# All four token tiles pass each stage of the layer together, and 66 blocks of the product with U run ahead of the first V block

## The chip, the cores and the metric

The kernel runs on one core of one Trainium2 chip. The metric is the device time of that core in microseconds. Of the kernel before three runs are shown: 1733.40, 1733.98 and 1734.52 us, median 1733.98.

## What is computed

One decoder layer of width 1024 on 512 tokens. Sub-layer 1 is a modulated norm, an input projection whose columns go to two groups of eight attention heads (a latent attention with rotary keys, and a forgetting attention), and an output projection. Sub-layer 2 is a product-key expert mixer, and nearly all of the time is spent there or on the way to it. Cut to what matters:

```python
h = modulate(x, norm1_g, shift1, scale1);  proj = h @ w_in            # 1024 wide
o = concat(latent_attention(proj), forgetting_attention(proj))        # 8 + 8 heads, causal
x = x + gate1 * (o @ w_o)
h2 = modulate(x, norm2_g, shift2, scale2)
qp = (h2 @ w_pq)                        # 8 heads x 2 halves x 128
sc = einsum("bshpd,hpnd->bshpn", qp, sub_keys)        # 128 keys for each half
s1, i1 = top_k(sc[..., 0, :], 16);  s2, i2 = top_k(sc[..., 1, :], 16)
top_s, top_c = top_k(s1[..., :, None] + s2[..., None, :], 16)
expert = i1[top_c // 16] * 128 + i2[top_c % 16];  gate = softmax(top_s)
a = einsum("bcd,bchkd->bchk", h2, peer_u[expert])     # 16384 experts x 1024
y = einsum("bchk,bchkd->bcd", gate * gelu(a), peer_v[expert])
x = x + gate2 * y
```

## The kernel before, in words

The 512 tokens are four tiles of 128. All products that need fp32 are made of three matmuls (`mm3`, L405): each operand is split into a rounded part `hi` and a rest `lo`. A weight is loaded in pieces of 128x1024; ScalarE casts `whi` (L397), and VectorE or GpSimd subtracts to `wlo` (L398). The `halves` of a weight are kept under the number of the pair of tiles (`i // 2`), so each weight is loaded and split once for tiles 0 and 1 and again for tiles 2 and 3.

The front has, for each tile: `hidden` (the norm, transposed), the base projections (`latent_q`, `latent_k`, `fox_qk` twice, `fox_v`; L409 to L411) and `mla_tile` (L193), sixteen `head`s (score L590, softmax, transposes L156, product with V L605), `out_proj`, `hidden2`. Then `queries` (with `w_pq`; L409 to L411 with `h2hi`) give the scores against the keys (L676 on), and `best` takes the sixteen best of 128 keys for each half (five VectorE instructions, L733 to L737). `choose` calls `select`, the pick: sums of candidates (L763), again a top-16, and a look-up of the expert's number (L779 on VectorE, L781 on GpSimd, L782 on VectorE).

Of the four tiles, three are dense and one is sparse. For the dense tiles `gate_matrix` turns the numbers and gates into a matrix G over all 16384 experts: one-hots on VectorE (L821 to L824), products on TensorE (L830), written to DRAM. Then all experts are computed, in 128 blocks of 128: `dense_u` (24 matmuls 128x384, L929 to L931, with `ut` split by `split`, L883 and L884) and `gelu` give `ge`, and `v_in` and `v_mm` multiply it by the gate (L962), split it (`whl`, L965, L966) and add 18 matmuls 128x512 (L975). A U block must come before its V block; `AHEAD = 20` blocks go first and the rest alternate with V. For the sparse tile, 3, `sparse_steps` gathers rows of U and V from DRAM (L841) and works on VectorE alone: 128 u-steps (L862) and 128 v-steps (L871), a few beside each V block.

Every engine takes its own instructions in order. That order comes from generators: `pipe` starts a task every few rounds, `weave` puts a number of steps of a second generator between steps of a first. The last part of `build` (L1070 to L1095) is the plan: tiles 0 and 1 up to their scores; then the picks and gates of tiles 0 and 1 as `fill` beside base projections and heads of tiles 2 and 3; then the output projections and queries of these; then picks and gates of tile 2 beside the first U blocks.

Of the kernel before, what the change touches and what calls it, by code (L numbers as in the profile page):

```python
# [21 lines left out]
P = 128  # L22
# [4 lines left out]
H = 8  # L27
# [19 lines left out]
AHEAD = 20  # L47
# [33 lines left out]
class Layer:  # L81
    def __init__(self, ctx, tc, I, out):
# [26 lines left out]

    def q4(self, shape, name, dt=F32):  # L110
        return self.q4p.tile(list(shape), dt, name=name, tag="q4")
# [84 lines left out]
    def setup(self):  # L196
# [25 lines left out]
        self.mask = cp.tile([P, S], F32, name="mask")  # L222
# [32 lines left out]
    def rope_tables(self):  # L255
# [34 lines left out]
        self.rope = {}  # L290
        for j, name in enumerate("qk"):
            g1 = rg[:, j * RD:j * RD + hf][:, None, :].to_broadcast([P, NT, hf])
            g2 = rg[:, j * RD + hf:(j + 1) * RD][:, None, :].to_broadcast([P, NT, hf])
            c = cp.tile([P, NT, RD], F32, name="rc_" + name)
            s = cp.tile([P, NT, RD], F32, name="rs_" + name)
# [42 lines left out]
    def mod_cols(self, j, name, bias, gain=None, first=False, halves=(0, 1)):  # L338
# [3 lines left out]
        for half in halves:  # L342
            alloc = self.g8 if not first else self.q4 if half == 0 else self.oh if gain is None else self.l4
# [38 lines left out]
    def weights(self, i, name, alloc):  # L382

        if (i // 2, name) not in self.wt:
            self.wt[i // 2, name] = self.wload(self.I[name], alloc)
        return self.wt[i // 2, name]

    def halves(self, i, name, src, engs, new=None):

        if (i // 2, name) not in self.wt:  # L390
# [10 lines left out]
            self.wt[i // 2, name] = his.__getitem__, los.__getitem__  # L401
        return self.wt[i // 2, name]
# [749 lines left out]
```

## Time and profile before

| | |
|---|---|
| median of three runs | 1733.98 us (1733.40 to 1734.52) |
| the profiled run, its own time | 1733.38 us |
| its span | 1731.6 us |
| TensorE matmul busy | 1607.5 us, 93% |
| VectorE busy | 1315.4 us, 76% |
| ScalarE busy | 706.9 us, 41% |
| GpSimd busy | 649.0 us, 37% |
| DMA | 414.93 MB, mean 240 GB/s |

A row of a window gives the stretch in us from the span's start, its length, and for TensorE (PE), its weight loads (PEld), VectorE (DVE), ScalarE (ACT) and GpSimd (POOL) the busy time with the number of instructions in brackets; then the granted TensorE clock as a share of the full one, the mean busy share of the DMA engines, and GB/s. A window of one line gives only the engines on which that line has instructions. A row of a group gives line, engine, operation, operands out<-in with their shapes and the count, then busy time and mean duration of one in ns, then the idle time just before them and what ended it. Busy time counts a moment once; means of overlapping instructions add up to more.

### The profile page before, as it was taken

The numbers are of one execution on the slowest core, as the hardware profiler recorded it, in microseconds if no ns is written. First come the engines' busy times: TensorE is split into PE (matmuls) and PEld (weight loads), VectorE is DVE, ScalarE is ACT, GpSimd is POOL, SyncE is SP. The second block draws the span as 40 slices with busy tenths as digits, with TensorE's granted clock in tenths as the row PEclk, the third lists the DMA queues.
The fourth block names the chain that finished last, engine by engine and source line by source line (L and its number), as shares of the span: only waits on it lengthen the run. The fifth ranks groups of instructions, "written<-read, shape, count | busy, mean of one in ns | idle before, by whom it ended". The sixth has DMA issues, their size and how long they took to land.

```text
span 1731.6 us, 25066 instructions
## 1 busy us (share of the span) xinstructions
PE 1607.5 (93%) x9105; PEld 1417.4 (82%) x9105; DVE 1315.4 (76%) x2762; ACT 706.9 (41%) x1100; POOL 649.0 (37%) x569
## 2 busy tenths in 40 slices
PE   7999878789879789779999999999999999999998
PEld 3758877569758689768889999999999999999987
DVE  4735669989898987877888888888888877445764
ACT  3435544259465246633333333333333333333331
POOL 1650735641432440373554444534534433001200
PEclk8999989889989899889999999999999999999999
DMA  8584454325276436868999999999999999445761
GB/s 298 182 307 147 144 172 152 100 74 169 76 250 202 145 97 202 261 242 281 341 341 348 354 323 342 339 331 348 325 337 356 314 336 353 132 159 178 260 200 67
DMA packets 160909, 414.93 MB, mean 240 GB/s; under 512 B 13201, under 2 KB 68497, under 8 KB 159250
## 3 DMA queue, kind: packets, MB, share of 16 engines
q1 hardware_dynamic: 64658, 242.85, 40.7%
q0 software_dynamic: 37440, 137.38, 22.0%
q10 hardware_dynamic: 58688, 33.11, 6.5%
q8 instruction: 71, 1.16, 0.3%
q14 instruction: 52, 0.43, 0.1%
HBM read 380.25 MB, written 33.03 MB: 239 GB/s over the span
## 4 chain that ended last, share of the span: by engine, by line
PE 69%; DVE 18%; DMA 3%; issue 3%; POOL 2%; ACT 2%; ACTq 0%; POOLq 0%; DVEq 0%
PE acc L975 30%; PE bank L931 9%; PE bank L929 9%; PE bank L930 9%; DVE wlo L398 2%; DVE idf L782 2%; PE bank L590 2%; PE bank L830 1%; PE bank L156 1%; PE bank L605 1%; PE bank L410 1%; PE bank L411 1%; PE bank L409 1%; DVE ti L737 1%; DVE sc L735 1%
## 5 line engine op out<-in xcount | busy, mean ns | idle before, releaser
L975 PE MATMUL acc<-vhi,whl 128*128 128x512 f32 x1524 | 435.9, 396 | 0.0
L929 PE MATMUL bank<-hhi,uhi 128*128 128x384 f32 x1024 | 346.9, 339 | 9.2 <-DMA hhi<-hd 6.5
L931 PE MATMUL bank<-hhi,ulo 128*128 128x384 f32 x1024 | 346.9, 339 | 6.3 <-DVE ulo L884 3.9
L930 PE MATMUL bank<-hlo,uhi 128*128 128x384 f32 x1024 | 346.4, 338 | 0.8 <-DMA hlo<-hd 0.8
L975 PEld LDWEIGHTS acc<-vhi,whl 128*128 128x128 f32 x1524 | 286.5, 189 | 57.5 <-issue 0.5
L841 POOL DMA_INDIRECT gat<-in_peer_v,ids x128 | 164.6, 1286 | 324.9 <-DVE y L871 150.5
L883 ACT CAST uhi<-ut 128x1024 fp32r<-128x1024 f32 x129 | 135.4, 1051 | 304.2 <-PE bank L930 301.6
L975 PE MATMUL acc<-vlo,whl 128*128 128x512 f32 x762 | 240.0, 396 | 10.4 <-POOL vlo L884 10.4
L841 POOL DMA_INDIRECT gat<-in_peer_u,ids x128 | 164.6, 1286 | 199.0 <-DVE sact L862 182.0
L884 DVE TENSOR_TENSOR ulo<-ut,uhi 128x1024 fp32r<-128x1024 f32 x124 | 153.3, 1237 | 110.6 <-ACT uhi L883 108.6
L883 ACT CAST vhi<-vt 128x1024 fp32r<-128x1024 f32 x127 | 133.3, 1050 | 234.3 <-PE acc L975 205.4
L884 DVE TENSOR_TENSOR vlo<-vt,vhi 128x1024 fp32r<-128x1024 f32 x122 | 149.7, 1227 | 81.1 <-ACT vhi L883 77.6
L929 PEld LDWEIGHTS bank<-hhi,uhi 128*128 128x128 f32 x1024 | 194.0, 190 | 14.9 <-issue 7.0
L931 PEld LDWEIGHTS bank<-hhi,ulo 128*128 128x128 f32 x1024 | 194.2, 190 | 9.4 <-DVE ulo L884 5.4
L930 PEld LDWEIGHTS bank<-hlo,uhi 128*128 128x128 f32 x1024 | 194.2, 190 | 5.6 <-DMA hlo<-hd 1.3
L975 PEld LDWEIGHTS acc<-vlo,whl 128*128 128x128 f32 x762 | 144.4, 190 | 44.9 <-POOL vlo L884 11.3
L871 DVE SCALAR_TENSOR_TENSOR y<-gat,swgt,y 128x1024 f32<-128x1024 f32 x127 | 162.4, 1279 | 19.0 <-DMA gat<-in_peer_v,ids 19.0
L398 POOL TENSOR_TENSOR wlo<-w,whi 128x1024 fp32r<-128x1024 f32 (+2 forms) x45 | 112.8, 2516 | 155.5 <-ACT whi L397 130.8
L862 DVE CUSTOM_DVE_ANT_0 scr<-gat,h 128x1024 bf16<-128x1024 f32 x128 | 155.9, 1218 | 14.2 <-DMA gat<-in_peer_u,ids 12.0
L965 ACT CAST whl<-ge 128x384 fp32r<-128x384 f32 x113 | 57.6, 512 | 138.8 <-DVE ge L962 120.8
L397 ACT CAST whi<-w 128x1024 fp32r<-128x1024 f32 (+2 forms) x88 | 84.8, 994 | 53.0 <-DMA w<-in_w_pq 10.4
L832 ACT ACTIVATE gst<-bank 128x512 f32<-128x512 f32 x96 | 95.0, 1083 | 24.2 <-PE bank L830 17.4
(278 smaller groups left out, 2620.4 us busy)
## 6 DMA issues: line engine op xcount, KB each, us to landing
ut<-in_peer_uT SPq DMA_DIRECT2D x128, 512.0 KB
vt<-in_peer_v SPq DMA_DIRECT2D x127, 512.0 KB
G<-gst ACTq DMA_DIRECT2D x24, 1024.0 KB
w<-in_w_pq SPq DMA_DIRECT2D x32, 512.0 KB
w<-in_w_ada SPq DMA_DIRECT2D x24, 512.0 KB
w<-in_w_ada SPq DMA_DIRECT2D x12, 1024.0 KB
w<-G SPq DMA_DIRECT2D x16, 768.0 KB
gt<-G SPq DMA_DIRECT2D x16, 768.0 KB
```

The source lines that it names most:

```text
L397: self.nc.scalar.copy(hi, w)
L398: engs[k // 2 % len(engs)].tensor_tensor(out=lo, in0=w, in1=hi, op=OP.subtract)
L832: nc.scalar.activation(st[:, :, q + t4:q + t4 + 4].rearrange("p i t -> p t i"), pb.rearrange("p (t i) -> p t i", t=4), AF.Copy, scale=1.0 ...
L841: self.nc.gpsimd.indirect_dma_start(out=t, out_offset=None, in_=self.I[table], in_offset=bass.IndirectOffsetOnAxis(ap=ids[:, k:k + 1], axi ...
L862: v.tensor_tensor_reduce(out=scr, in0=u, in1=h2, op0=OP.mult, op1=OP.add, scale=1.0, scalar=0.0, accum_out=a[:, k:k + 1])
L871: v.scalar_tensor_tensor(out=self.y, in0=t, scalar=w[:, k:k + 1], in1=self.y, op0=OP.mult, op1=OP.add)
L883: nc.scalar.copy(hi, src)
L884: eng.tensor_tensor(out=lo, in0=src, in1=hi, op=OP.subtract)
L929: pe.matmul(A, uh[:, k, :], hh, start=(k == 0), stop=False)
L930: pe.matmul(A, uh[:, k, :], hl, start=False, stop=False)
L931: pe.matmul(A, ul[:, k, :], hh, start=False, stop=(k == KD - 1))
L975: self.nc.tensor.matmul(self.acc[t][half], w[:, ts], v[:, half * 512:(half + 1) * 512], start=(b == n == 0), stop=(b == NK - 1 and n == 2))
```

## The change

Weights are kept under their name alone, so each is loaded and split once (44 pieces of 128x1024 in place of 88), those of `w_in` and `w_pq` all on VectorE. All four tiles go through each stage together, and one pool of 28 buffers replaces four pools. The queries take four tiles at once: 384 matmuls of 512 columns in place of 768 of 256. The sixteen calls of `top` stand, one for each step of the queries, after the first five steps. Then the U blocks begin (`ahead`), one for every two steps of the six picks of tiles 0 to 2 and one for every step of their gates; 66 of them in place of 20 are made before the loop over V. The `ge` of blocks 15 to 65 is stored to DRAM (`ged`) and loaded again three V blocks ahead (`ge_in`). The loop over V takes 1 or 2 sparse steps per block up to block 60, and 3 from there (before: 1 up to block 15, then 2 or 3). All `ulo` and `vlo` splits are on VectorE (before, five of each on GpSimd).

```diff
 EARLY = 15
-AHEAD = 20
+AHEAD = 66
...
-        self.k4p = self.top.enter_context(tc.tile_pool(name="k4", bufs=12))
-        self.q4p = self.top.enter_context(tc.tile_pool(name="q4", bufs=8))
-        self.w4p = self.top.enter_context(tc.tile_pool(name="w4", bufs=4))
-        self.l4p = self.top.enter_context(tc.tile_pool(name="l4", bufs=4))
+        self.k4p = self.top.enter_context(tc.tile_pool(name="k4", bufs=28))
...
-    def halves(self, i, name, src, engs, new=None):
-
-        if (i // 2, name) not in self.wt:
...
+    def halves(self, name, src, engs, new=None):
+
+        if name not in self.wt:
             kd, n = src.shape[1:]
             his, los = [], []
             for k in range(0, kd, 2):
-                w = self.w4([P, 2, n], "w")
+                w = self.k4([P, 2, n], "w")
                 self.last_load = self.nc.sync.dma_start(w, src[:, k:k + 2, :])
-                hi, lo = (new or self.q4)([P, 2, n], "whi", F32R), self.l4([P, 2, n], "wlo", F32R)
+                hi, lo = (new or self.k4)([P, 2, n], "whi", F32R), self.k4([P, 2, n], "wlo", F32R)
                 self.nc.scalar.copy(hi, w)
                 engs[k // 2 % len(engs)].tensor_tensor(out=lo, in0=w, in1=hi, op=OP.subtract)
                 his += [hi[:, x, :] for x in range(2)]
                 los += [lo[:, x, :] for x in range(2)]
-            self.wt[i // 2, name] = his.__getitem__, los.__getitem__
-        return self.wt[i // 2, name]
+            self.wt[name] = his.__getitem__, los.__getitem__
...
-    def w_in(self, i, name):
-
-        v, g = self.nc.vector, self.nc.gpsimd
-        new = {"w_c0": self.oh, "w_c1": self.oh, "w_fq": self.k4, "w_fv": self.oh}.get(name) if i > 1 else None
-        return self.halves(i, name, self.I[name], (g, g, v) if i > 1 else (v, g), new)
+    def w_in(self, name):
+
+        return self.halves(name, self.I[name], (self.nc.vector,), self.oh if name in ("w_c1", "w_fq") else None)
...
-    def w_pq(self, i, c):
-        v, g = self.nc.vector, self.nc.gpsimd
-        return self.halves(i, f"w_pq{c}", self.I["w_pq"][c], (v,) if c == 0 else (v, g))
+    def w_pq(self, c):
+        return self.halves(f"w_pq{c}", self.I["w_pq"][c], (self.nc.vector,), self.oh if c % 2 else None)
...
-        qT = (self.oh([P, 4, n], "qpT", F32) if group[0] == 0 else self.k4([P, 4, n], "qpT"))
+        qT = [self.k4([P, 2, n], "qpT") for _ in range(2)]
         for j in range(4):
             pb = self.bank()
             self.mm3(pb[:, :n], [lambda k, z=z: w[z](k)[:, j * P:(j + 1) * P] for z in range(2)], h, KD)
-            self.ecopy(qT[:, j, :], pb[:, :n], j)
+            self.nc.scalar.copy(qT[j // 2][:, j % 2, :], pb[:, :n])
...
-            nc.gpsimd.tensor_tensor(out=lo, in0=src, in1=hi, op=OP.subtract)
+            nc.vector.tensor_tensor(out=lo, in0=src, in1=hi, op=OP.subtract)
...
-                late = i == DENSE[-1] and q
+                late = q
...
+    def ahead(self):
         self.ge = {}
         self.acc, self.vs = None, {}
         self.dense_h2()
-        u = AHEAD
         for b in range(AHEAD):
             self.dense_u(b)
             yield
+
+    def dense(self):
+
+        u = AHEAD
         for b in range(NK):
+            self.ge_in(b + 3)
             self.v_in(b)
...
-        return self.split(ut, "u", self.nc.gpsimd if b % 2 and b < 11 else self.nc.vector)
+        return self.split(ut, "u", self.nc.vector)
...
+        if EARLY <= b < AHEAD:
+            nc.sync.dma_start(self.ged[b - EARLY], self.ge.pop(b))
+
+    def ge_in(self, b):
+
+        if EARLY <= b < AHEAD:
+            self.ge[b] = self.k2([P, ND_T], "ge")
+            self.load(self.ge[b], self.ged[b - EARLY])
...
-        vh, vl = self.split(vt, x, nc.gpsimd if b < 5 else nc.vector)
+        vh, vl = self.split(vt, x, nc.vector)
...
-        h0, h1 = hiddens([0, 1])
+        every = list(range(NT))
+        hs = hiddens(every)
         for x in ("a1", "b1", "a2", "b2"):
             self.mods[x] = self.cp.tile([P, KD], F32, name=x)
         m = [f for half in range(2) for f in (self.mod_cols(0, "b1", 0, None, True, (half,)),
                                               self.mod_cols(1, "a1", 1, 4, True, (half,)))]
+        h0, h1 = hs[:2]
         for g in (m[0], h0, h1, m[1], m[0], m[2], m[1], m[3], m[2], m[3], h0, h1):
             next(g, None)
         self.tables()
-        weave(pipe(base([0, 1]) + self.heads(0, T) + self.heads(1, T), 3),
-              spread(seq(self.mod_row(2, "g1", 0, self.k4, self.g8), spill(), self.mod_cols(3, "b2", 2), self.mod_cols(4, "a2", 3, 5)), 2), 1, 8)
-        b23, o01 = base([2, 3]), outs([0, 1])
-        run(pipe(o01[:3] + hiddens([2, 3]) + o01[3:] + seconds([0, 1]) + b23[:4] + [prep(self.w_pq, 0, 0)], 3))
-        weave(seq(*scores([0, 1])), seq(top(0, 0), top(1, 0), idle(2), top(0, 1), top(1, 1), pick(0, 0), top(0, 2)), 1, 5)
-        fill = seq(top(1, 2), top(0, 3), pick(0, 1), top(1, 3), gates(0), pick(1, 0), pick(1, 1), gates(1))
-        weave(pipe(b23[4:] + self.heads(2, T) + self.heads(3, T), 2), fill, 1)
-        run(pipe(outs([2, 3]) + [prep(self.w_pq, 2, 0)] + seconds([2, 3]), 2))
-        weave(seq(*scores([2, 3])), seq(top(2, 0), top(3, 0), idle(2), top(2, 1), top(3, 1), pick(2, 0), top(2, 2)), 1, 5)
-        dense = self.dense()
-        next(dense)
-        weave(seq(top(2, 3), pick(2, 1)), dense, 1, 0, 1, False)
-        for _ in range(4):
-            next(dense)
-        weave(gates(2), dense, 1, 1, 2, False)
-        sparse = seq(top(3, 2), top(3, 3), behind(pick(3, 0)), behind(pick(3, 1)), self.sparse_steps(SPARSE))
+        weave(pipe(hs[2:] + base(every) + self.heads(0, T) + self.heads(1, T), 3),
+              spread(seq(self.mod_row(2, "g1", 0, self.k4, self.g8), spill(), self.mod_cols(3, "b2", 2), self.mod_cols(4, "a2", 3, 5)), 2), 1, 10)
+        o = outs((0, 0), (1, 0), (2, 0), (0, 1), (1, 1), (2, 1), (3, 0), (3, 1))
+        run(pipe(self.heads(2, T) + self.heads(3, T) + o + [prep(self.w_pq, 0)] + seconds(every), 2))
+        tops = [top(i, c) for c in range(4) for i in every]
+        weave(seq(*scores(every)), seq(*tops), 1, 5)
+        ahead = self.ahead()
+        next(ahead)
+        weave(seq(*(pick(i, hh) for i in DENSE for hh in range(2))), ahead, 1, 0, 2, False)
+        weave(seq(*(gates(i) for i in DENSE)), ahead, 1, 0, 1, False)
+        run(ahead)
+        sparse = seq(behind(pick(3, 0)), behind(pick(3, 1)), self.sparse_steps(SPARSE))
         g2 = spread(self.mod_row(5, "g2", 1, self.o4, self.o4, True), 5)
-        for n, _ in enumerate(dense):
-            for _ in range(1 if n < 16 else 3 if n % 2 else 2):
+        for n, _ in enumerate(self.dense()):
+            for _ in range(3 if n >= AHEAD - 5 else 1 + n % 2):
                 next(sparse, None)
```

What this does to the order of VectorE's instructions shows at two places. The first is where the first U block's rest, `ulo` (L884 before, L870 after), stands among candidates (L733 to L737 before, L719 to L723 after, `sc` scores), look-ups (`lk`, `idf`) and one-hots (L807 to L810 after). Before:

```order
L763 TENSOR_TENSOR cand<-tv 128x4x2 x3
L734 MAX_INDEX ti<-tv,sc 128x8
L737 MAX_INDEX ti<-tv,sc_6360 128x8
L884 TENSOR_TENSOR ulo<-ut,uhi 128x1024
L779 TENSOR_TENSOR lk<-io_299,tpf 128x800
L734 MAX_INDEX ti<-tv,sc 128x8 x3
L735 MATCH_REPLACE sc_6366<-tv,sc 128x128
L782 TENSOR_REDUCE idf<-lk 128x16
L736 MAX tv<-sc_6366 128x8
```

And after, at the first `ulo`:

```order
L768 TENSOR_REDUCE idf<-lk 128x16
L723 MAX_INDEX ti<-tv,sc_4484 128x8
L809 TENSOR_TENSOR vhi<-vt,e_5577 128x1024
L810 TENSOR_TENSOR vhi<-vt,e_5577 128x1024
L722 MAX ts<-c_5451 128x8
L809 TENSOR_TENSOR vhi<-vt,e_5577 128x1024
L810 TENSOR_TENSOR vhi<-vt,e_5577 128x1024
L870 TENSOR_TENSOR ulo<-ut,uhi 128x1024
L770 CAST ids_4876<-idf 128x64
L765 TENSOR_TENSOR lk<-io_291,tpf 128x800
L870 TENSOR_TENSOR ulo<-ut,uhi 128x1024
```

Before, the first top-16s of tiles 2 and 3 stand on both sides of the first `ulo`, and those of tiles 0 and 1 far ahead of it. After, all 64 first top-16s (the last ends with the `MAX_INDEX` of `sc_4484`), 24 second ones (`c`), 16 look-ups and five steps of one-hots stand ahead of it. By TensorE's order 68 U blocks stand ahead of the first V matmul, behind one group of 16 one-hot matmuls (before, 24 by the trace).

The second place is VectorE in the loop over V: before, one V block with its U block and three sparse steps (L862 is a u-step, an `ISA` of two instructions, L871 a v-step):

```order
L871 SCALAR_TENSOR_TENSOR y<-gat,swgt,y 128x1024
L884 TENSOR_TENSOR vlo<-vt,vhi 128x1024
L862 ISA scr,sact<-gat,h_8273 128x1024
L862 ISA sact 128x1
L966 TENSOR_TENSOR whl<-ge,whl 128x384
L871 SCALAR_TENSOR_TENSOR y<-gat,swgt,y 128x1024
L884 TENSOR_TENSOR ulo<-ut,uhi 128x1024
L962 TENSOR_TENSOR ge<-ge,w_10735 128x192
L962 TENSOR_TENSOR ge<-ge,w_10736 128x192
L862 ISA scr,sact<-gat,h_8273 128x1024
L862 ISA sact 128x1
```

And after, between V block 6 and 60 (L870 is the split, L848 and L857 the sparse steps, L960 and L964 the gate and `whl`):

```order
L960 TENSOR_TENSOR ge<-ge,w_9914 128x192
L960 TENSOR_TENSOR ge<-ge,w_9915 128x192
L870 TENSOR_TENSOR vlo<-vt,vhi 128x1024
L848 ISA scr,sact<-gat,h_8939 128x1024
L848 ISA sact 128x1
L964 TENSOR_TENSOR whl<-ge,whl 128x384
L857 SCALAR_TENSOR_TENSOR y<-gat,swgt,y 128x1024
```

The `ulo` is gone from there, since U blocks 0 to 69 stand ahead of V block 6 and the next comes at V block 60, and each V block comes with one u-step and one v-step. From V block 78 on the order is that of before.

## Rows read from the trace of the kernel before

**Rows 1.** The whole span, cut into stages, all engines (windows).

```profile
0.00:227.00 227.00, 193.93 (x1103) 146.19 (x1103) 123.30 (x328) 108.35 (x245) 95.64 (x111) 0.94 0.63 220
20.00:200.00 180.00, 164.61 (x948) 124.23 (x941) 106.87 (x279) 90.27 (x204) 77.12 (x79) 0.96 0.60 211
227.00:592.70 365.70, 308.95 (x2366) 276.60 (x2365) 334.04 (x1070) 183.46 (x296) 154.29 (x143) 0.93 0.45 141
592.70:738.20 145.50, 128.70 (x836) 122.53 (x837) 119.89 (x347) 73.85 (x93) 40.11 (x48) 0.92 0.62 194
738.20:1731.60 993.40, 975.94 (x4805) 872.11 (x4804) 738.17 (x1020) 341.19 (x466) 359.01 (x269) 0.99 0.81 287
```

**Rows 2.** Queries and first top-16s: count, ns min/median/max, first and last start.

```profile
L409 PE MATMUL bank<-h2hi,whi x256: 278/283/561, 227.0 to 579.9; 128*128 128x256 f32 x128
...
L733 DVE MAX8 tv<-sc x64: 266/274/296, 244.6 to 589.1; 128x8 f32<-128x128 f32 x64
```

**Rows 3.** The chain in the steady stretch: start, us, what.

```profile
1463.60 4.18 PE acc L975 x18
...
1471.97 4.18 PE acc L975 x18
```

**Rows 4.** TensorE's timeline, runs of small matmuls: start, us, what.

```profile
164.78 1.50 PE L605 MATMUL bank<-V,pT 128*128 128x128 f32 x12
...
208.58 1.03 PE L156 MATMUL bank<-ident,xn 128*128 128x128 f32 x8
...
658.37 0.92 PE L830 MATMUL bank<-vhi,vt 128*128 128x128 f16 x13
```

**Rows 5.** Candidates and picks of tiles 0 and 1, all engines (window).

```profile
244.00:350.00 106.00, 91.25 (x531) 76.24 (x530) 104.12 (x477) 34.19 (x50) 66.25 (x73) 0.94 0.39 129
```

**Rows 6.** VectorE's groups in that stretch, six of thirty.

```profile
L398 DVE TENSOR_TENSOR wlo<-w,whi 128x1024 fp32r<-128x1024 f32 x8 | 14.7, 1839 | 0.3 <-ACT whi L397 0.3
L782 DVE TENSOR_REDUCE idf<-lk 128x16 f32<-128x800 f32 x8 | 12.0, 1505 | 0.0
L763 DVE TENSOR_TENSOR cand<-tv 128x8 f32<-128x8 f32 (+5 forms) x36 | 11.3, 356 | 0.0
L736 DVE MAX8 tv<-sc 128x8 f32<-128x128 f32 x32 | 9.1, 285 | 0.4
...
L779 DVE TENSOR_TENSOR lk<-io,tpf 128x800 f16<-128x800 f16 x8 | 5.1, 654 | 0.0
...
L734 DVE MATCH_VALUE_LOAD ti<-tv,sc 128x8 f32 x32 | 2.3, 72 | 0.0
```

**Rows 7.** VectorE's groups of the dense part and of the gates, whole span.

```profile
L871 DVE SCALAR_TENSOR_TENSOR y<-gat,swgt,y 128x1024 f32<-128x1024 f32 x127 | 162.4, 1279 | 19.0 <-DMA gat<-in_peer_v,ids 19.0
L862 DVE CUSTOM_DVE_ANT_0 scr<-gat,h 128x1024 bf16<-128x1024 f32 x128 | 155.9, 1218 | 14.2 <-DMA gat<-in_peer_u,ids 12.0
...
L884 DVE TENSOR_TENSOR vlo<-vt,vhi 128x1024 fp32r<-128x1024 f32 x122 | 149.7, 1227 | 81.1 <-ACT vhi L883 77.6
...
L966 DVE TENSOR_TENSOR whl<-ge,whl 128x384 fp32r<-128x384 f32 x113 | 62.3, 553 | 13.9 <-ACT whl L965 13.9
...
L962 DVE TENSOR_TENSOR ge<-ge,gt 128x192 f32<-128x192 f32 x112 | 35.7, 363 | 0.0
...
L821 DVE TENSOR_TENSOR o<-io,e 128x1024 f16<-128x1024 f16 x40 | 31.5, 787 | 5.1 <-PE bank L830 5.1
```

**Rows 8.** The steady stretch, 100 us and 20 us of it (windows).

```profile
1000.00:1100.00 100.00, 100.00 (x505) 90.66 (x504) 84.32 (x118) 35.39 (x50) 45.75 (x36) 1.00 0.93 328
...
980.00:1000.00 20.00, 20.00 (x99) 17.77 (x99) 15.10 (x22) 6.89 (x10) 7.12 (x7) 1.00 1.00 388
```

**Rows 9.** The products of `mla_tile` on TensorE, whole span (groups).

```profile
L193 PE MATMUL bank<-w,lT 128*128 128x384 f32 (+1 forms) x80 | 32.4, 555 | 5.2 <-ACT V L507 3.5 <-DVE qa L521 1.7
```

**Rows 10.** U matmuls (L929, one of three lines) ahead of the V stage (window).

```profile
0.00:738.20 738.20, 67.22 (x192) 37.76 (x192) 0.93 0.54 176
```

**Rows 11.** The first U blocks, beside picks and gates of tile 2 (window).

```profile
592.70:640.00 47.30, 40.95 (x203) 39.37 (x204) 41.11 (x150) 15.71 (x21) 21.13 (x21) 0.87 0.44 143
```

More of the change, by code (lines that the diff above doesn't have):

```diff
@@ L342, in mod_cols @@
         for half in halves:
-            alloc = self.g8 if not first else self.q4 if half == 0 else self.oh if gain is None else self.l4
+            alloc = self.k4 if first else self.g8
             acc = self.mod_parts(self.wload(self.I["w_ada"][j, half], alloc))
@@ L379, in normed_T, with weights @@
         self.transposes([h[:, k * P:(k + 1) * P] for k in range(KD)], self.scaled(dst, a, b))
-    def weights(self, i, name, alloc):
-        if (i // 2, name) not in self.wt:
-            self.wt[i // 2, name] = self.wload(self.I[name], alloc)
-        return self.wt[i // 2, name]
-    def halves(self, i, name, src, engs, new=None):
-        if (i // 2, name) not in self.wt:
+    def weights(self, name, alloc):
+        if name not in self.wt:
+            self.wt[name] = self.wload(self.I[name], alloc)
+        return self.wt[name]
+    def halves(self, name, src, engs, new=None):
+        if name not in self.wt:
             kd, n = src.shape[1:]
@@ L435, in times_h @@
     def times_h(self, pb, i, T, name):
-        self.mm3(pb, [lambda k, z=z: T["hT"][z][:, k, :] for z in range(2)], self.w_in(i, name), KD)
+        self.mm3(pb, [lambda k, z=z: T["hT"][z][:, k, :] for z in range(2)], self.w_in(name), KD)
     def latent_q(self, i, T):
@@ L495, in mla_tile @@
     def mla_tile(self, i, T):
-        wuq, wkv = self.weights(i, "w_uq", self.w4), self.weights(i, "w_ukv", self.l4)
+        wuq, wkv = self.weights("w_uq", self.k4), self.weights("w_ukv", self.k4)
         nc = self.nc
@@ L625, in heads, with w_o @@
         return [self.head(i, T, g, h) for g in (1, 0) for h in range(H)]
-    def w_o(self, i, half):
-        return self.halves(i, f"w_o{half}", self.I["w_o"][half], (self.nc.vector, self.nc.gpsimd))
+    def w_o(self, half):
+        return self.halves(f"w_o{half}", self.I["w_o"][half], (self.nc.vector, self.nc.gpsimd))
     def out_proj(self, i, T, half):
@@ L634, in out_proj @@
             self.load(self.x[i], self.I["x"][i * P:(i + 1) * P, :])
-        w = self.w_o(i, half)
-        if i == 2 and half == 0:
+        w = self.w_o(half)
+        if i == half == 0:
             self.mods["g1"] = self.k4([P, D], "g1")
@@ L658, in queries @@
         G = T[group[0]]
-        w = self.w_pq(group[0], c)
-        h = [lambda k, z=z: G["h2"][z][k // 4][:, k % 4, :] for z in range(2)]
+        w = self.w_pq(c)
+        h = [lambda k, z=z: G["h2"][z][k // 2][:, k % 2, :] for z in range(2)]
         keys = self.k2([P, 4, NK], "keys")
         self.load(keys, self.I["keys"][c])
-        qT = (self.oh([P, 4, n], "qpT", F32) if group[0] == 0 else self.k4([P, 4, n], "qpT"))
+        qT = [self.k4([P, 2, n], "qpT") for _ in range(2)]
         for j in range(4):
@@ L702, in hidden2 @@
         if i == group[0]:
-            new = self.q4 if i else self.k4
-            T[i]["h2"] = [[new([P, KD // 2, len(group) * P], x, F32R) for _ in range(2)] for x in ("h2hi", "h2lo")]
+            T[i]["h2"] = [[self.k4([P, 2, len(group) * P], x, F32R) for _ in range(KD // 2)] for x in ("h2hi", "h2lo")]
         ts = slice(group.index(i) * P, (group.index(i) + 1) * P)
@@ L885, in split @@
         return hi, lo
-    def dense(self):
+    def ahead(self):
         self.ge = {}
@@ L1014, in hiddens, with outs @@
             return [self.hidden(i, T[i]) for i in group]
-        def outs(group):
-            return [self.out_proj(i, T[i], half) for half in range(2) for i in group]
+        def outs(*which):
+            return [self.out_proj(i, T[i], half) for i, half in which]
         def seconds(group):
```

39 lines of the change are left out of this document (18 added, 21 removed).

## The prediction

> **What bounds the kernel now.** I first cut the span at its stages [rows 1]. Up to the first query matmul of tiles 0 and 1 [rows 2] TensorE is busy 193.9 of 227.0 us (of its 33 us of idle, 15 stand in the 180 us of projections and heads from 20 on). From there to the first U block it is busy 309.0 of 365.7 us while VectorE is busy 334.0: there the candidates and gates of tiles 0 and 1 run beside the projections and heads of tiles 2 and 3. From 592.7 to the first V block TensorE is busy 128.7 of 145.5 us, and then 975.9 of 993.4 us. So TensorE sets the pace nearly everywhere; over the four stages it is not busy for 124 us (33 + 57 + 17 + 17), and part of the busy time before 738 us was run at a granted clock of 0.92 to 0.94. What the change does is therefore counted in TensorE's idle time: it wins where it removes some of the 124, and loses where it puts in new.
>
> Second, the unit prices. In the steady stretch a U block and a V block together come every 1471.97 - 1463.60 = 8.37 us, of which the V block's 18 matmuls take 4.18 [rows 3]; a U block is thus 4.19, a matmul of 512 columns 0.232 and one of 384 0.174 (296 columns: 0.134, by columns). From runs of small matmuls [rows 4], less the duration of the last one: a half of an fp32 128x128 product 0.11, a transpose 0.11, a one-hot matmul 0.058.
>
> Third, VectorE's work in candidates and gates [rows 5, 6], and what VectorE and the DMA queues do per block in the dense part [rows 7, 8]: where TensorE gets less work beside them, these become the pace.
>
> **Part 1: the front for four tiles at once.** It does not get shorter in sum: the queries need all four tiles, so their first matmul moves behind the work of tiles 2 and 3, which stood after it. Added on TensorE: base projections of two tiles, 2 x 24 x (3 x 0.232 + 0.174 + 0.134) = 48.2, less 14.8 for the 96 matmuls with `w_c0` and `w_c1` that already stood ahead of the queries = 33.4; `mla_tile`, half of 32.4 = 16.2 [rows 9]; 112 blocks of heads (16 heads x 3 and 4 key blocks) x (0.22 score + 0.11 transpose + 0.22 PV) = 61.6; output projection 96 x 0.232 = 22.3; some 114 other transposes x 0.11 = 12.5. Sum 146 by these prices, which are those of full clock and no gap. At the busy share of the stretch from 20 to 200 us, which has the same kinds of work (164.6 of 180 [rows 1]), it would be 160; I take the middle, 153, so that the first query matmul comes at 227 + 153 = 380. The 44 pieces of weights that are no longer split a second time (on VectorE 1.84 us each where GpSimd splits beside it [rows 6], and GpSimd's share) gain nothing in my sum: TensorE's matmuls in the front cover them, and without that cover they would cost in both kernels alike. Bounds: 327 if all 33 us of idle and the lost clock of the first 227 us (0.94, some 13 us) went; 400 if the added work ran at the busy share that it has in the second stage of before (309 of 366).
>
> **Part 2: queries and candidates, with nothing beside them.** The queries of four tiles are 384 matmuls of 512 columns, 89 us. The first scores come after a quarter of the queries (22.3) and about 5 us more for copies and scores (before it took 17.6 us to the first top-16, with queries half as long [rows 2]), at 407. From there VectorE has, in its order ahead of the first `ulo` split that the U blocks need: 64 first top-16s x 1.58 us (the eight groups of a top-16 sum to 50.6 for 32, the longest and the shortest are in [rows 6]) = 101; 24 second ones x 1.1 = 27; 54 `cand` additions x 0.314 = 17; 16 `idf` x 1.5 = 24; 17 hits x 0.64 = 11; 12 weight splits x 1.23 = 15 (the duration without GpSimd beside it, of the same shape [rows 7]); five one-hot steps of four operations x 0.79 [rows 7] = 15; small ones 11. That is 221 us by group sums. In the stretch of before that does this same work, the groups sum to 128.2 us for 104.1 us busy in 106 us of time [rows 5], since neighbours overlap: a factor of 0.81, thus 179 busy, less 4 splits that come before the first scores, and 178 with VectorE's own gaps (106/104). Low end 160 (the splits and one-hots hide wholly in gaps), high end 221 (no overlap, as when each step of a top-16 waits for the one before). I take 178, the same instructions in the same mix. The first `ulo` is then done at about 585, and TensorE's order has nothing between the scores and the U blocks but 16 one-hot matmuls: of the 205 us from the first query matmul on it works some 107 (scores: 64 products of two halves x 0.11 = 14), and waits for 98. This is the change's largest cost. Before, the same VectorE work stood beside heads.
>
> **Part 3: 68 U blocks ahead of the first V block** (before: 24, which is the 192 matmuls of [rows 10] over 8). 68 x 4.19 = 285; the one-hot products of 43 steps x 16 x 0.058 = 40 stand in between; 3 for transposes of the gates, and 6 for the ping-pong between VectorE, GpSimd and TensorE at its start (before, the stretch 592.7 to 640 lost 6.4 us of TensorE and ran at 0.87 [rows 11]). Sum 334. VectorE has about 235 us here, so it is covered. The `ge` stores queue on SP behind the `gelu` of their block; `ut` loads stand three to four blocks ahead of each store in SP's order, so I cost them at zero (low end 0, high end 1 us a block, rival 3). The first V block is then at 585 + 334 = 919.
>
> **Part 4: the V stage.** Before: 104 x 8.37 + 24 x 4.18 = 971, and 993.4 - 971 = 22 for start and end. After: 60 x 8.37 + 68 x 4.18 = 786, + 22 = 808, if TensorE still set the pace everywhere. It does not: from V block 6 to 60 no U block stands on VectorE, while each V block comes with one u-gather and one v-gather step. Per such block VectorE has `vlo` 1.23, `ge` 2 x 0.36, `whl` 0.55, the u-step 1.22 and the v-step 1.28 [rows 7] = 5.00 by means; before, a pair of blocks with two splits and three steps sums to 7.49 by the same rows and fills 84.3 of 100 us, at 8.37 a pair 7.06 [rows 8], a factor of 0.94, so 4.7. The DMA queues carry per block 512 KB of `vt`, 192 of `ge` reloaded (new), 192 of G and 2 x 512 of gathers = 1.966 MB. At the highest rate that before shows over 20 us, 388 GB/s at a share of 1.00 [rows 8], that is 5.07 us; at the 328 of 100 us with share 0.93, 5.57 at full share. TensorE's 4.18 is the least of the three. I take 5.1, thus 54 x (5.1 - 4.18) = 50 more, between 28 (VectorE alone) and 75 (the lower rate). V stage 808 + 50 = 858.
>
> On this rate the Trainium skill ("DMA: Bandwidth & Descriptors", section Specifications) names a limit of about 358 GB/s from HBM for a core, and its measured table, with the other core of the pair idle, 425. The 388 of this trace lies above the first, so the measurement decides against it here; by 358 a block would be an estimated 5.5 us and the sum some 20 us longer, by 425 an estimated 4.6, under VectorE's, and 20 us shorter.
>
> **Sum.** 380 + 205 + 334 + 858 = 1777 us of span; 3 more for low clock where TensorE starts again after the 98 us (the first U blocks of before ran so [rows 11]); the profiled run has 1.8 us outside its span (1733.4 against 1731.6) and stands 0.6 under the median of the three runs, 1734.0. Forecast 1782. Against before: idle 98 (candidates), 50 (V only), 40 (front) and 31 (ping-pong, start, end) for the 124, and about 50 us back because the work before the dense part is priced near full clock.
>
> **Rivals.**
> 1. Faster: the front was held up by the splits, by GpSimd beside VectorE and by the switching of two pairs of tiles, and with four tiles in one pipeline it runs without a hole. For it: 33 us of idle and a clock of 0.94 in the first row, and `wlo` on VectorE at 1.84 us against 1.23 of the same shape. Against it: the same kinds of work from 20 to 200 us left 15 us idle with all splits of tiles 0 and 1 paid once, as now [rows 1]. With the first query matmul at 327 the time is 1782 - 53 = 1729; it beats before from about 330 down, or from 352 if the V-only stretch also stays at its low bound.
> 2. The DMA queues top out at the lower rate in the V-only stretch: 5.57 a block, +25, 1807. For it: the row of 100 us does not reach 388. Against it: TensorE was full there, so it asked for no more. The other way, VectorE alone sets it: 1760.
> 3. The `ge` stores hold up SP: a store waits for its `gelu`, and if the next `ut` load is queued behind it, each U block of the 51 that store gains about 1 us: +51, 1833. SP's order speaks against it.
> 4. The clock: TensorE waits 18% of the V-only stretch. In [rows 11] a stretch with 13% of idle shows a granted 0.87; at 0.87 a V block's matmuls last 4.8, still under 5.1. At the lower of its two levels, 1.2 GHz, they would last 8.4 and the stretch would cost 54 x 3.3 = 178 more: 1960. Against it: in the steady rows of before the clock stays at 1.00 [rows 8], though none has a gap in every block. The Trainium skill ("TensorE: Matmul & The Clock Gate", section What's actually happening) has a lack of activity throttle the array, which speaks for it; [rows 11] agrees in kind.
>
> **How the numbers follow.** Forecast with its own terms (1748 to 1806): 0.66. Rival 1, alone or with the low V-only bound: 0.14 (1705 to 1740), of which 0.11 is faster by more than 0.2%, the bound of what can be told from no change here. Rival 2's high side: 0.10. Rival 3: 0.06. Rival 4: 0.04. Faster 0.12, same 0.03, slower 0.85. The range goes from 1724 (into rival 1) to 1830 (rival 2 and most of 3), which leaves out about 2 in 10.
>
> **What would show it.** The first query matmul at 365 to 400; a hole of 80 to 115 us on TensorE between the last scores and the U blocks, with VectorE over 95% busy in it; 68 U blocks in some 335 us with TensorE full; from V block 6 to 60 a cadence of 5.1 with the DMA share near 1.00, and 8.37 a pair after it. Wrong: a front under 335, U matmuls inside the candidates' stretch, or a V-only cadence of 4.2.

## The result and the profile after

The changed kernel takes 1836.88 us (median of four, 1835.47 to 1841.98) against 1733.69 of the kernel before: a ratio of 1.0607, 95% interval 1.0578 to 1.0636, 103 us slower. The forecast was 1782 with a range to 1830: the sign was right, the size was not, and the time lies outside the range. The profiled execution took 1835.47 us, its span 1833.7.

The stages of the changed kernel as windows, in the columns of [rows 1], which they answer to:

```profile
0.00:388.70 388.70, 338.91 (x2050) 273.49 (x2050) 175.67 (x528) 162.88 (x384) 83.86 (x126) 0.94 0.37 130
388.70:493.20 104.50, 104.47 (x516) 88.33 (x515) 78.11 (x373) 29.48 (x48) 8.67 (x15) 0.98 0.23 76
493.20:598.90 105.70, 4.59 (x22) 2.98 (x22) 103.70 (x487) 4.92 (x11) 36.84 (x68) 0.51 0.07 23
598.90:945.00 346.10, 333.00 (x2351) 321.66 (x2352) 222.36 (x383) 190.85 (x235) 20.63 (x33) 0.98 0.69 211
945.00:967.20 22.20, 7.29 (x37) 6.97 (x36) 19.03 (x28) 3.60 (x5) 9.53 (x7) 0.73 0.91 311
...
967.20:1833.70 866.50, 812.73 (x3748) 687.90 (x3748) 676.54 (x977) 279.28 (x382) 351.02 (x263) 0.98 0.86 310
```

Their borders are starts from the lines themselves (count, ns min/median/max, first and last start), the first two the answer to [rows 2]:

```profile
L397 PE MATMUL bank<-h2hi,whi x128: 387/389/794, 388.7 to 488.8; 128*128 128x512 f32 x128
...
L719 DVE MAX8 tv<-sc x64: 273/276/295, 420.2 to 502.5; 128x8 f32<-128x128 f32 x64
...
L870 DVE TENSOR_TENSOR ulo<-ut,uhi x129: 1209/1225/2568, 598.9 to 1797.4; 128x1024 fp32r<-128x1024 f32 x129
...
L973 PE MATMUL acc<-vhi,whl x1524: 387/395/794, 967.2 to 1824.8; 128*128 128x512 f32 x191
```

TensorE's busy time is almost that of before, 1601.0 against 1607.5 us. Its idle time went from 124 to 233 us, and that is the whole loss. By stages: 50 before the first query matmul, 101 between the scores and the first `ulo`, 28 from there to the first V matmul, 54 in the V stage (span less busy time in each row).

TensorE's timeline over the largest hole (start, us, what, and in brackets the idle time before it with what ended it):

```profile
489.44 3.73 PE L661 MATMUL bank<-keys,qpT 128*128 128x128 f32 x32
561.21 0.90 PE L789 MATMUL bank<-ident,e 128*128 128x128 f32 x3 [68.04 <-DVE e L784]
578.08 0.37 PE L816 MATMUL bank<-ohl,o 128*128 128x128 f16 x2 [15.96 <-DVE ohl L809]
578.77 1.65 PE L816 MATMUL bank<-ohl,o 128*128 128x128 f16 x14 [0.33 <-DVE ohl L810]
596.05 0.98 PE L919 MATMUL bank<-hhi,uhi 128*128 128x384 f32 x2 [15.63 <-DMA hhi<-hd]
...
600.66 0.53 PE L919 MATMUL bank<-hhi,uhi 128*128 128x384 f32 x1
600.98 0.53 PE L920 MATMUL bank<-hlo,uhi 128*128 128x384 f32 x1
```

VectorE is busy 103.7 of these 105.7 us. Note what releases the first U matmul: not a split, but the load `hhi<-hd`, whose tile lies in memory that the front's pool of 28 buffers held until then (e1 and e2 bear this out). From 600.7 to 605.1 us the matmuls start 0.32 us apart, not 0.174: the granted clock is still at the lower of its two levels there (0.50), after the row in which TensorE worked 4.6 of 105.7 us.

### The profile page after: what moved, and what is told of

It reads as the page before. It is cut to its first block, busy times and chain, and to the rows that moved or that the text cites. A ratio compares the mean times of both kernels' runs of the same rounds, so it can differ in the third digit from the quotient of the medians.

```text
span 1833.7 us, 24343 instructions
## 1 busy us (share of the span) xinstructions
PE 1601.0 (87%) x8721; PEld 1381.3 (75%) x8721; DVE 1275.4 (70%) x2769; ACT 671.0 (37%) x1062; POOL 510.5 (28%) x510
## 5 line engine op out<-in xcount | busy, mean ns | idle before, releaser
L973 PE MATMUL acc<-vhi,whl 128*128 128x512 f32 x1524 | 438.6, 402 | 44.1 <-ACT vhi L869 29.1
L973 PEld LDWEIGHTS acc<-vhi,whl 128*128 128x128 f32 x1524 | 289.2, 192 | 115.1 <-ACT vhi L869 38.2
L973 PE MATMUL acc<-vlo,whl 128*128 128x512 f32 x762 | 245.5, 404 | 17.5 <-DVE vlo L870 17.1
L870 DVE TENSOR_TENSOR ulo<-ut,uhi 128x1024 fp32r<-128x1024 f32 x129 | 159.5, 1236 | 128.2 <-ACT uhi L869 126.7
L827 POOL DMA_INDIRECT gat<-in_peer_u,ids x128 | 171.0, 1336 | 209.6 <-DVE sact L848 189.4
L973 PEld LDWEIGHTS acc<-vlo,whl 128*128 128x128 f32 x762 | 142.4, 191 | 63.8 <-DVE vlo L870 33.9
L857 DVE SCALAR_TENSOR_TENSOR y<-gat,swgt,y 128x1024 f32<-128x1024 f32 x127 | 162.6, 1280 | 33.2 <-DMA gat<-in_peer_v,ids 33.2
L870 DVE TENSOR_TENSOR vlo<-vt,vhi 128x1024 fp32r<-128x1024 f32 x127 | 155.5, 1225 | 42.0 <-ACT vhi L869 40.3
L848 DVE CUSTOM_DVE_ANT_0 scr<-gat,h 128x1024 bf16<-128x1024 f32 x128 | 155.9, 1218 | 12.7 <-DMA gat<-in_peer_u,ids 12.3
L749 POOL TENSOR_TENSOR cid<-tif 128x8 f32<-128x8 f32 (+5 forms) x72 | 19.0, 299 | 431.6 <-DVE tif L740 431.5
L397 PE MATMUL bank<-whi,hTh 128*128 128x512 f32 (+2 forms) x160 | 58.8, 387 | 14.7 <-ACT whi L385 14.7
```

The source lines that it names most:

```text
L397: pe.matmul(pb, lh, rh, start=(k == 0), stop=False)
L827: self.nc.gpsimd.indirect_dma_start(out=t, out_offset=None, in_=self.I[table], in_offset=bass.IndirectOffsetOnAxis(ap=ids[:, k:k + 1], axi ...
L848: v.tensor_tensor_reduce(out=scr, in0=u, in1=h2, op0=OP.mult, op1=OP.add, scale=1.0, scalar=0.0, accum_out=a[:, k:k + 1])
L857: v.scalar_tensor_tensor(out=self.y, in0=t, scalar=w[:, k:k + 1], in1=self.y, op0=OP.mult, op1=OP.add)
L870: eng.tensor_tensor(out=lo, in0=src, in1=hi, op=OP.subtract)
L973: self.nc.tensor.matmul(self.acc[t][half], w[:, ts], v[:, half * 512:(half + 1) * 512], start=(b == n == 0), stop=(b == NK - 1 and n == 2))
```

## The experiments

The theory after the result: (1) the hole comes from the scores' buffers, which hold the U blocks back; (2) the V-only stretch is slow for the gathers beside the `vt` loads; (3) splitting once saved nothing; (4) the wait before the first V matmul is the gate matrix on its way through DRAM. The rivals stand in each expectation. Ratios are to the kernel before, run beside each.

**Scores through DRAM (e1).**

```diff
-                self.sc = self.k4([P, 2, 4, NK], "sc")
-            sc = T[i]["sc", c] = self.sc[:, a % 2]
+            sc = self.k2([P, 4, NK], "sc")
             nc.scalar.copy(sc.rearrange("p a b -> p (a b)"), pb)
+            nc.sync.dma_start(self.scd[4 * i + c], sc)
...
+        T["sc", c] = self.k2([P, 4, NK], "sc")         # in best()
+        self.load(T["sc", c], self.scd[4 * i + c])
```

> The changed kernel with one thing altered: the scores go through DRAM and come back into a small pool just before their top-16, instead of lying in the 28 buffers until then. Theory (the scores' buffers are the ones that the U blocks need, so the first U block waits until the last top-16 has read them, and TensorE waits about 100 us for VectorE's candidates, picks and first one-hots): the first ulo moves ahead of most of that work in VectorE's order, the first U matmul comes at 500 to 515 us instead of 596, VectorE becomes the bound of the stretch beside the U blocks (some 326 us of work left at 493 us), the first V matmul comes at 850 to 880 instead of 967, time about 1740 (1715 to 1765). Rival (VectorE's work itself must be done before U blocks are of use, or the load of the second norm's result is late for another reason): first U matmul after 580, time within 10 us of 1836.

Measured 1778.8 us, ratio 1.0244 (1.0207 to 1.0282). Ahead of the first `ulo` VectorE has 894 instructions in place of 1385. Starts of the first U and V matmuls, then the stretches beside the candidates:

```profile
L920 PE MATMUL bank<-hhi,uhi x1024: 331/334/735, 504.3 to 1749.0; 128*128 128x384 f32 x171
...
L974 PE MATMUL acc<-vhi,whl x1524: 387/395/796, 913.7 to 1769.7; 128*128 128x512 f32 x191
```

```profile
504.00:600.00 96.00, 80.20 (x413) 77.14 (x413) 94.31 (x433) 31.65 (x43) 26.51 (x47) 0.91 0.45 145
600.00:700.00 100.00, 89.24 (x553) 84.76 (x554) 91.95 (x165) 46.97 (x59) 31.07 (x29) 0.95 0.54 164
```

The first U matmul comes 92 us earlier, as expected; the first V matmul only 53.5, not the 87 to 117 expected, since VectorE (94.3 of 96 us) now paces both. So the buffers make the hole, and VectorE's work keeps about half of it. This accounts for 58 of the 103 us.

**Half of the top-16s (e2).**

```diff
+            if j % 2 == 0:
                 self.top16(...)
+            else:
+                self.nc.vector.tensor_copy(T["tv"][:, h, z], T["sc", c][:, j, :TOPK])
+                self.nc.vector.tensor_copy(T["ti"][:, h, z], T["ti"][:, h, 0])
```

> The changed kernel with half of the 64 first top-16s left out (every second one is replaced by two short copies). Theory (the hole on TensorE between the scores and the first U block ends when VectorE has done its list, and nothing else is late): 32 x (1.58 - 0.25) x 0.81 = 34 us less in the hole, time 1796 to 1806. Rival (the hole ends with a load or with a buffer that comes free for another reason): less than 10 us gained.

Measured 1783.3 us, ratio 1.0277. The gain is 53, not 34, and the first U matmul comes 73 us earlier, at 523.5:

```profile
L923 PE MATMUL bank<-hhi,uhi x1024: 331/334/735, 523.5 to 1750.2; 128*128 128x384 f32 x171
```

The list alone would give 34. The top-16s are what reads the scores, so fewer of them free the buffers sooner, and picks and one-hots move behind the first U block (6 of the 16 `idf` look-ups are left ahead of the first `ulo`, and no one-hot): this fits e1, and the expectation had the wrong mechanism.

**One sparse step per V block (e3).**

```diff
-            for _ in range(3 if n >= AHEAD - 5 else 1 + n % 2):
+            for _ in range(3 if n >= AHEAD - 5 else 1):
```

> The changed kernel with one sparse step per V block up to block 60 in place of one and two in turn. Theory (in the stretch of V blocks without U blocks, the two gathers of 512 KB per block set the pace through the DMA queues): 1.45 MB a block, under TensorE's 4.18 us at any rate seen, so the cadence there falls from 5.39 to 4.2 to 4.3 us, 55 to 60 us less, and the steps that move behind block 60 find room there (3 per pair of 8.37 us): time 1775 to 1790. Rival a (the reload of ge and its way through the queue set the pace): the cadence stays above 5 us, time above 1815. Rival b (the moved steps lengthen the pairs behind block 60): cadence 4.2 first, pairs over 8.6 later, time 1790 to 1815.

Measured 1875.3 us, ratio 1.0813: 38 slower than the changed kernel. The edit did not do what it says. The planner that orders the instructions pulled later steps forward, and VectorE's order has 2 steps per V block there, as in the changed kernel (24 from block 24 to 36 in both). What it did is leave 36 steps (6 in the changed kernel) for after V block 120, where TensorE stands, so it says nothing of what sets the cadence. The end of e3:

```profile
1800.00:1872.80 72.80, 28.02 (x115) 21.75 (x113) 49.52 (x57) 4.81 (x8) 32.26 (x28) 0.73 0.67 216
```

**Without the reload of `ge` (e4).**

```diff
-            self.load(self.ge[b], self.ged[b - EARLY])
+            self.nc.scalar.copy(self.ge[b], self.hhi[0][:, 0, :].bitcast(F32))
```

> The changed kernel without the reload of ge from DRAM (ScalarE copies other data from SBUF into the same tile, so the values are not those of the layer; the stores stay). Theory (DMA bytes set the V-only cadence of 5.39 us at about 360 GB/s): 192 of some 1920 KB less, cadence 4.85 to 4.95, 22 to 28 us less, time 1808 to 1815. Rival (waits of the sparse steps on one another, or VectorE, set it): cadence 5.3 to 5.4, time within 6 us of 1836.

Measured 1818.6 us, ratio 1.0481, 18 us less (two runs, 10 us apart). A V block is 18 matmuls, so the 869 of L973 in this stretch are 48.3 blocks, 5.07 us each, where the changed kernel has 5.39 (918 in 275 us, at 360 GB/s and a share of 0.97). All engines of e4 in that stretch (its 869 matmuls are all of L973):

```profile
1000.00:1245.00 245.00, 215.87 (x869) 164.91 (x868) 216.40 (x336) 95.67 (x144) 128.26 (x97) 0.97 0.95 349
```

The bytes fell by 10%, the cadence by 6%, less than bytes alone gave (4.85 to 4.95). The edit takes the reload's places in SP's queue away together with its bytes, so which of the two counted is not shown.

**Paced steps (e5, e6).** Every step is tied to its V block; e6 has `1` in place of `1 + n % 2`.

```diff
-            for _ in range(3 if n >= AHEAD - 5 else 1 + n % 2):
-                next(sparse, None)
+            with self.tc.issue_after(self.last_v.ins):     # vlo of this V block
+                for _ in range(3 if n >= AHEAD - 5 else 1 + n % 2):
+                    next(sparse, None)
```

> The changed kernel with its sparse steps tied to the V blocks: each of the one or two steps of a block may only be issued after the vlo split of that block, so that VectorE's order has 1.5 steps per V block up to block 60 (78 by there) in place of 2 (112 by there), and the rest stands later, where the changed kernel has a stretch of some 50 us without steps; the last step still stands ahead of the last V block. Theory (the gathers' bytes on the DMA queues set the V-only cadence): 1.69 in place of 1.94 MB a block, at 350 to 360 GB/s 4.7 to 4.8 us in place of 5.39, 30 to 35 us less over 54 blocks; time 1800 to 1808. Rival (the wait of vt loads and the reload of ge in SP's queue sets it, not the bytes): cadence above 5.2, time above 1825.

> As the kernel with paced steps, but one step per V block up to block 60 (48 by there); some 22 steps are left behind the last V block. Theory (bytes): 1.43 MB a block is 4.0 us at 355 GB/s, less than TensorE's 4.18, so the V-only cadence falls to 4.2 to 4.3 us and TensorE has hardly a gap in it; the steps left at the end cost 35 to 50 us there, so the whole time is 1815 to 1835. Rival (VectorE or ge's reload sets the V-only cadence): it stays above 4.8.

Measured 1816.0 (ratio 1.0460, 1.0430 to 1.0489) and 1844.7 us (1.0625; its steps left over lie at the end). The V-only cadence of e5, 857 matmuls in 250 us, is 5.25:

```profile
1000.00:1250.00 250.00, 213.47 (x857) 167.61 (x858) 195.48 (x314) 76.40 (x103) 98.45 (x76) 0.92 0.90 325
```

and of e6, 825 in 220 us, 4.80:

```profile
1000.00:1220.00 220.00, 201.20 (x825) 158.83 (x824) 158.65 (x260) 70.48 (x95) 54.12 (x50) 0.96 0.85 297
```

Both cadences miss what bytes alone gave (4.7 to 4.8, and 4.2 to 4.3), and the DMA share falls to 0.90 and 0.85: the queues are not full and TensorE still waits. What SP's queue waited for from 1000 to 1275 us in the changed kernel (total us, times, longest) shows a second cause:

```profile
SPq L291 <- DVE vlo L870: 142.6, 50, 5.6
SPq L291 <- DVE whl L964: 47.1, 22, 4.7
```

A `vt` load is issued only when the `vlo` split two blocks earlier has freed one of its two buffers; landing, cast and split then stand in a chain.

**Splitting twice (e7).**

```diff
-                engs[k // 2 % len(engs)].tensor_tensor(out=lo, in0=w, in1=hi, op=OP.subtract)
+                for _ in range(1 if name.startswith("w_pq") else 2):
+                    engs[k // 2 % len(engs)].tensor_tensor(out=lo, in0=w, in1=hi, op=OP.subtract)
```

> The changed kernel with the subtraction for wlo of the 28 weight pieces of w_in and w_o done twice over (the same result), about 34 us more work on VectorE and GpSimd in the front. Theory (TensorE sets the front's time, so splitting the weights once saved nothing there): first query matmul within 6 us of 388.7, time within 8 us of 1836.9. Rival (the splits set the front's time): first query matmul 15 to 34 us later, time 1852 to 1871.

Measured 1839.3 us, ratio 1.0594 against 1.0607. The first query matmul comes at 395.8, 7 us later (1 beyond the theory's bound) for 34 us more of splits on VectorE (67.0 us of `wlo` ahead of it in place of 33.2) and 11 more on GpSimd, and the whole time is the same. Subtracting once is worth little; casts and loads were not doubled.

**Both gains together (e8)**: the diffs of e1 and e5.

> The changed kernel with both edits, scores through DRAM and paced sparse steps. Theory: the two gains stand in different stretches and add up: 1778.8 - 32 = 1747 (1738 to 1758), still over the kernel before, since the front up to the first query matmul takes 388 us and the stretch of candidates beside U blocks is VectorE's. Rival (the gains overlap, the DMA queues being the bound of the whole V stage): above 1765.

Measured 1764.1 us, ratio 1.0164 (1.0127 to 1.0201), 17 above the expectation, most of it the 11 by which e5's gain missed the 32 that were put in. It is the fastest version tried, and slower than the kernel before.

**Four `vt` buffers (e9), and with the other edits (e10, e11).**

```diff
-        x = "uv"[b < NK - 1]
+        x = "uv"[b < NK - 1 and not (b % 2 and 6 < b < AHEAD - 10)]
...
-        return self.split(ut, "u", self.nc.vector)                                        # e11 only
+        return self.split(ut, "u", self.nc.gpsimd if b % 2 and b < 26 else self.nc.vector)
```

> The changed kernel with four buffers in place of two for vt and its halves in V blocks 7 to 55: every second block uses those of ut, which lie idle there. Order and bytes otherwise as in the changed kernel (two sparse steps per block, 1.94 MB). Theory 1 (a vt load is issued only when the vlo split two blocks earlier has freed its buffer, and the way from there over the landing, ScalarE and VectorE to TensorE takes most of two blocks, so with the gathers beside it the loads come late): the cadence falls from 5.39 to 5.0 to 5.1 us, the 388 GB/s of the kernel before, some 15 us less, 1818 to 1826. Theory 2 (bytes at about 360 GB/s alone): cadence 5.3 to 5.4, time 1832 to 1840. Theory 3 (only the buffers, bytes not at all): 4.2 to 4.7, time below 1805.

> The changed kernel with scores through DRAM, paced steps and four vt buffers. With 1.69 MB a block and loads that come in time the V-only cadence should fall from 5.25 to 4.4 to 4.6 us: 35 to 45 us less than the 1764 of the first two edits, 1719 to 1732, about as the kernel before (1734 to 1737). If the bytes at 350 to 360 GB/s bind, 4.7 to 4.8 and 1738 to 1745; if something else (ge's reload in SP's queue), 5.2 and 1760.

> As the kernel with the three edits, and every second ulo split of the first 26 U blocks on GpSimd. Theory (VectorE sets the pace of the U blocks beside candidates and picks, where it was busy 186 of 196 us): 13 splits of 1.23 us less on VectorE in that stretch, 10 to 16 us less than the kernel with three edits. Rival (GpSimd's split takes 2.5 us and slows VectorE's beside it, as with wlo before, 1.84 us against 1.23): no gain, or up to 8 us lost.

Measured 1815.0 (ratio 1.0451), 1773.8 (1.0223) and 1779.8 us (1.0255). In e9 TensorE is full in the V-only stretch; all engines:

```profile
1000.00:1250.00 250.00, 250.00 (x1099) 205.61 (x1098) 200.91 (x321) 88.74 (x123) 89.16 (x68) 1.00 0.95 346
```

Its 1012 V matmuls there are 56.2 blocks in 236.2 us busy, 4.2 each. But the edit was not clean: the planner, seeing faster blocks, put 1.0 step beside each in place of 2. Its cadence is theory 3's, its time no theory's. It is to be compared with e6, also at 1.0 but with its steps tied to the blocks: 4.80 with two buffers, 4.2 with four. The tie is not the reason, since e10 has it too, and from 1000 to 1150 us, again at 1.0 step, TensorE is full in it:

```profile
1000.00:1150.00 150.00, 150.00 (x644) 120.70 (x643) 120.97 (x201) 53.40 (x74) 43.76 (x37) 1.00 0.96 356
```

So at equal steps the buffers bound e6, not the bytes; for the changed kernel's 2 steps the shares of the two causes stay open.

The mean cadences hide what the buffers have to bridge. The gates of eight V blocks come in two loads of 768 KB, one behind the other in SP's queue. In the changed kernel five such pairs were issued from 1043 to 1219 us, and 13 to 15 us after each TensorE waited 2.5 to 4.5 us for the cast of a late `vt`, in all 20 of the 39 us that it is idle from 1000 to 1275. One of them (SP's queue, ScalarE, TensorE):

```profile
1087.29 0.80 SPq L291 DMA_DIRECT2D w<-G  x2
1088.69 0.33 SPq L291 DMA_DIRECT2D vt<-in_peer_v  x1
1099.26 1.04 ACT L869 CAST vhi<-vt 128x1024 fp32r<-128x1024 f32 x1 [2.36 <-DMA vt<-in_peer_v]
1100.36 2.93 PE L973 MATMUL acc<-vhi,whl 128*128 128x512 f32 x6 [4.01 <-ACT vhi L869]
```

With four buffers and one step a block these waits are gone (e9, e10).

e10 as a whole reaches its expected cadence (798 matmuls in 200 us, 4.51) and still loses 10 us to e8, because the steps go to the end:

```profile
1600.00:1778.00 178.00, 135.49 (x629) 118.39 (x627) 129.57 (x171) 41.08 (x59) 66.42 (x51) 0.89 0.75 258
```

TensorE stands 42 us there, in e8 9 of the last 160. e11 gains nothing: a split takes GpSimd 2.43 us, and VectorE's beside it 1.37 in place of 1.24; TensorE did 159.4 us of work from 504 to 700, with e10's order 168.7.

**78 U blocks ahead (e12).**

```diff
-AHEAD = 66
+AHEAD = 78
```

> The changed kernel with 78 U blocks ahead in place of 66, so that by TensorE's order nine U blocks stand between the last one-hot product and the first V matmul, in place of two. Theory (the 22 us before the first V matmul, in which TensorE worked 7, are the way of the last part of the gate matrix: ScalarE, store to DRAM, load, product with ge on VectorE, and only TensorE work that stands there covers them): seven more U blocks cover that way, TensorE's wait for the first whl falls from 14.9 us to under 3, and so the 77 U blocks ahead take some 20 us less than 77 x 4.19 and the rest would; the twelve V blocks that now come without a U block cost 12 x 1.2 = 14 more, so the whole time is 1828 to 1838. Rival (that wait is for VectorE's picks of tile 3 or for the first vt, which move along with the first V block): the wait stays above 10 us, time 1845 to 1855.

Measured 1856.0 us, ratio 1.0690: just past the rival's range. The waits of the changed kernel on TensorE from 900 to 1010 us (engine, line, what it waited for: us in total, times, longest):

```profile
PE acc L973 <- ACT whl L963: 14.9, 1, 14.9
PE acc L973 <- DVE vlo L870: 7.4, 1, 7.4
```

and those of e12:

```profile
PE bank L921 <- DVE ulo L870: 13.5, 3, 8.9
```

The wait for the first `whl` is gone, as the theory has it, but U blocks now wait for `ulo` in the same place, where VectorE has the picks of tile 3. The longest of these `ulo` stands right behind a look-up of tile 3 that waited for GpSimd:

```profile
978.79 1.49 DVE L768 TENSOR_REDUCE idf<-y 128x16 f32<-128x800 f32 x1 [6.28 <-POOL y L767]
```

From 599 us to the first V matmul TensorE is idle 28 us in the changed kernel and still some 23 in e12. The hole has two causes, one behind the other; e5, where part of those picks stands later in VectorE's order, brings the first V matmul only 5 us forward (962.3).

## Why the prediction was right in sign and wrong in size

- **The front (380).** 388.7. TensorE's added work was right: 193.9 + 146 = 340 busy, measured 338.9. Its idle time is 50 us, not 40; 19 of it stand from 350 to 400, where the second norm of the last tile has nothing beside it. That splitting once gains nothing held for the subtraction (e7).
- **The candidates (205 us, of which 98 idle).** VectorE took 178.7 us from the first top-16 (420.2) to the first `ulo` (598.9); the forecast was 178. It began 13 us late, 9 from the front and 4 from the first scores. TensorE waited 101. The size was right, and the cause incomplete: the order of VectorE was read as given, but it is so because the scores lie in buffers that the U blocks need (e1, e2).
- **68 U blocks (334): the step that failed.** It took 368.3. TensorE worked 340 us in place of 328: the one-hot products were 47 groups at 0.99 us in the steady part, not 43 at 0.93 (five groups stand ahead of the U blocks in VectorE's order, but one in TensorE's), and the start ran at half the clock. The rest is idle time: 28 us, not 6, and 14.9 of them are one wait for the first `whl`, ahead of the first V matmul, which was in no term. "VectorE has about 235 us here, so it is covered" held as a sum (it worked 241) and failed at this place. The gate product that makes this `whl` needs a part of G that is loaded only after its store to DRAM (SP waited 8.5 us for it), and it stands in VectorE's order behind look-ups of tile 3 (`idf`, `h`):

```profile
950.04 0.38 SPq L291 DMA_DIRECT2D gt<-G  x1
958.91 1.47 DVE L768 TENSOR_REDUCE idf<-y 128x16 f32<-128x800 f32 x1
960.31 0.56 DVE L765 TENSOR_TENSOR h<-io,tpf 128x800 f16<-128x800 f16 x1
960.89 3.57 DVE L960 TENSOR_TENSOR w<-w,gt 128x192 f32<-128x192 f32 x8
967.21 1.22 PE L973 MATMUL acc<-vhi,whl 128*128 128x512 f32 x2 [14.92 <-ACT whl L963]
```

Of the 68 U blocks only two stand behind the last one-hot product, and TensorE was through with them at 952. Before, U blocks covered this way: the last one-hots ended at 717, the first V matmul came at 738.2, and TensorE waited only here in between:

```profile
728.03 0.52 PE L929 MATMUL bank<-hhi,uhi 128*128 128x384 f32 x1 [2.49 <-ACT ge L938]
```

So neither the 17 us idle of that row in [rows 1] nor the lump of 22 us "for start and end", which counts from the first V matmul on (10.4 of it are waits for `vlo` splits on GpSimd), had this wait in it; it could be read from where the last one-hots stand in TensorE's order.
- **The V stage (858).** 866.5. The V-only cadence was 5.39, not 5.1, 16 us over 54 blocks; the rest came out 8 under. That is the side of rival 2, at 360 GB/s. The argument from bytes named one cause of two: the two `vt` buffers were in no sum (e6, e9, e10), and G was put in at a mean of 192 KB a block, where it comes as 1.5 MB at every eighth.
- **The clock.** The V-only stretch kept 0.98, so the clock of rival 4 did not fall. Rival 3 neither: `ut` loads stayed ahead of the stores, and from 625 to 925 us TensorE's waits are 1.8 us in all, none of them for a U block. Rival 1 was the wrong way.

All four steps came out longer than forecast: 9 + 5 + 34 + 8.5, less the 3 added for the restart, is the 54 us between 1780 and 1833.7. The upper bounds of the steps lie 20 (front), 43 (candidates) and 25 us (V-only) over their terms, and the range let in 48 of these 88; the step that failed had no upper bound but rival 3.

What stays open: how the 5.39 us divide between bytes and buffers at two steps per block; how the 14.9 us divide between G's way through DRAM and the look-ups of tile 3; and whether a plan exists in which neither the gate matrix nor the picks of tile 3 hold up the first V block.

## What to carry to other kernels

Batching all tiles through each stage saves repeated set-up only where the repeated work was on the path; here it lay under TensorE, and the change gave up what had filled the gaps, namely one pair's candidates beside the other pair's heads. Before an early start is counted on, look at who holds its buffers: a pool that closes late moves the whole order of every engine behind its last reader. And a stretch that loses one of two alternating streams must be priced by the chain of its loads (issue, landing, cast, split) over its buffers and by the bursts that get in between, not by mean bytes alone.

## What the runs showed that was not expected

The DMA queues were not a fixed limit: the same stretch ran at 297 GB/s with TensorE waiting (e6) and at 346 with TensorE full (e9). The planner answered every change of the steps' rate or of the buffers with another order (e3, e9, e10), so an edit of a rate is not an experiment until the order shows it.
